# A hybrid decoder layer on one core: low halves of weights kept in DRAM for the second token half, gate operands made one step ahead, gather rates raised

## The chip, the cores and the metric

One core of a Trainium2 chip runs the whole layer. The metric is device time of one execution in microseconds, the median of three runs. Lower is better.

## What is computed

One decoder layer over 1024 tokens of width 1024, in float32:

- `x += concat(differential attention, mLSTM) @ w_out`, with four heads each; their inputs come from one projection `rms_norm(x) @ w_in` in 128-wide column blocks (29 of them with the gates' block).
- `x += PEER(rms_norm(x))`: per token and each of 8 retrieval heads, a query (`@ w_query`, 16 blocks) is matched with two sets of 128 keys; the best 16 of the 16 x 16 sums name 16 of 16384 experts. Each expert has a row of 1024 in `expert_u` and in `expert_v`: `y = sum_k g_k * gelu(x . u_k) * v_k`, so 128 experts per token.
- `x += sigmoid(rms_norm(x) @ w_ple_gate) * (p @ w_ple_proj)`, then a last RMSNorm.

## The kernel before

**Split numbers.** A float32 product is built of three matmuls. Each operand is split into a high half (ScalarE's copy to the rounded type `F32R`) and a low half (VectorE's subtraction of the high half). `mm3s` (line 140) issues hi x hi, hi x lo and lo x hi.

**Two token halves.** `front(0)` and `front(1)` (line 220) work on 512 tokens each: projection, attention, mLSTM, output projection, queries and top-k. Each of the two reads all 53 weight blocks of 512 KB (29 of `win`, 8 quarters of `wout`, 16 of `wq`) by `weight` (line 190), which loads the block on SP's queue, makes `whi` on ScalarE and `wlo` on VectorE. There are three buffers of `wraw` and two each of `whi` and `wlo`. In `project` and in the query stage all matmuls with the high half come ahead of those with the low half.

**The retrieval, done in two ways.** For 3 of the 8 token tiles the expert rows are gathered (`sparse`, line 831): 24 units of 16 steps; a step gathers one row per token of `expert_u` (`ru`, 512 KB) and of `expert_v` (`rv`) on GpSimd's queue and makes one pass over each on VectorE (lines 843 and 861), with the second table one unit behind the first: 400 steps. For the other 5 tiles it is dense: `dense_up` (line 944) multiplies with all of `expert_u` in 128 rows and applies Gelu into `ga_s` in DRAM; `gate_blocks` (line 891) builds the dense gate matrix `g_s` in DRAM; `dense_down` (line 1005) multiplies both and then with `expert_v`, four rows at a time in 32 groups. `tail` (line 1111) does the last part, a tile at a time in the order `TORD`; the last tile is tile 2, the last of the gathered ones, whose result it loads from `x3_s` (line 1124).

**Pacing.** The gathered part is a generator: 14 steps of top-k, then 400 steps. `pump(x)` (line 212) adds `x` to a debt and draws one step per whole number, at a lowered priority. It is called in the second token half only (`F_RATE`: per projection block, per query block but the last five, per output quarter), per row of the up stage (`UP_RATE`: the first value for 40 rows, then the second), per row of the down stage (`DOWN_RATE`), and in the tail until the generator is empty. `anchor` names an instruction, and `behind` orders the passes after it in the schedule without a semaphore. The rows gathered land in a ring of buffers, 3 deep in the front, 4 in the up stage, 6 in the down stage and 2 from row 108 of the down stage on (`FLUSH`).

**Gate products.** The last 42 of the top-k's steps take one row each of the up stage; from then on `gate_blocks` draws 80 steps, spread over the rows so that it ends near row 119. A block of 16 tokens is two steps: four VectorE operations make one-hot matrices (`o1`, `w0`, `o1` again, `o0`, lines 918 to 922, one buffer each), ScalarE reorders a half of them into `wc` (line 927, one buffer), TensorE makes 16 matmuls into `pg` (line 931), and ScalarE copies into `st` (line 934), which goes to DRAM when 32 tokens are full.

The order on each engine is made ahead of time by a scheduler that goes by priority (the order of the program, shifted by `high_priority`) and modelled times; on the chip each engine and queue then runs in that order.

## Time and profile before

| what | value |
|---|---|
| three runs | 3117.79, 3124.81, 3115.04 us; median 3117.79 |
| the profiled execution's own time | 3123.69 us |
| its span, first to last instruction | 3121.9 us |
| TensorE busy (matmul) | 2873.4 us, 92% |
| VectorE busy | 2557.4 us, 82% |
| ScalarE, GpSimd busy | 1317.8 us (42%), 1007.6 us (32%) |
| mean granted TensorE clock | 0.965 |
| moved by DMA | 829.01 MB, mean 266 GB/s |

Busy time is the time in which an engine executes instructions, whatever it waits for later; a matmul's end is modelled. The chain of waits goes back from the last instruction, at each step to what released it. The second token half runs from about 475 to 992 us of the span, the up stage to 1988, the down stage to about 2905, and the tail to the end.

### The profile page before, as it was taken

The page shows a single profiled execution, that of the slowest core. Times are in us where ns is not written, and L with a number is a line of the kernel's source. Part 1 is how long each engine was busy: PE and PEld are TensorE (multiplying, and loading weights), DVE is VectorE, ACT ScalarE, POOL GpSimd, SP SyncE. Part 2 cuts the span into 40 slices and gives each one's busy share as a digit, 9 for nine tenths or more (in the row PEclk, how much of TensorE's full clock was granted, in tenths as well). Part 3 has the DMA queues.
Part 4 walks back from the last instruction along what each step waited for, and adds up shares of the span by engine and source line. Part 5 has one row for each costly group of instructions (what it writes and reads, how often), then busy time and mean ns, then how long its engine had stood idle before and what let it go on. Part 6 is the DMA issues. An engine that isn't in the chain of part 4 may idle for free.

```text
span 3121.9 us, 44819 instructions
## 1 busy us (share of the span) xinstructions
PE 2873.4 (92%) x16367; PEld 2517.4 (81%) x16367; DVE 2557.4 (82%) x5349; ACT 1317.8 (42%) x2152; POOL 1007.6 (32%) x786
## 2 busy tenths in 40 slices
PE   7999989998697999999999999899989999998894
PEld 6887868776586999998889999778768888887773
DVE  5565889888799889799999797678778888888795
ACT  5664336655222222487776565212222222232241
POOL 0000000334414333444444555434333444414431
PEclk9999989999898999999999999899999999999997
DMA  5333433777846787899999989999989999988763
GB/s 168 100 111 127 150 126 93 233 229 244 303 133 233 264 276 244 306 345 340 343 340 346 370 328 367 372 348 340 313 291 330 339 333 329 338 295 276 259 222 124
DMA packets 316797, 829.01 MB, mean 266 GB/s; under 512 B 26144, under 2 KB 115104, under 8 KB 314016
## 3 DMA queue, kind: packets, MB, share of 16 engines
q0 software_dynamic: 112608, 410.04, 37.6%
q1 hardware_dynamic: 185536, 374.16, 34.9%
q10 hardware_dynamic: 18432, 41.95, 3.5%
q8 instruction: 128, 2.10, 0.3%
q14 instruction: 93, 0.76, 0.1%
HBM read 715.43 MB, written 102.24 MB: 262 GB/s over the span
## 4 chain that ended last, share of the span: by engine, by line
PE 55%; DVE 15%; DMA 12%; issue 12%; ACT 3%; POOL 2%; another core or an unknown queue 0%; SPq 0%; DVEq 0%; ACTq 0%; POOLq 0%
PE A L145 23%; PE mm L145 12%; PE keep L145 5%; DMA raw<-in_vr 4%; DMA rv<-in_ev,eidx 3%; DVE ya L861 3%; PE S L145 2%; DVE ru L843 2%; PE pg L931 2%; PE Y L136 2%; PE Y L137 2%; PE Y L138 2%; DVE tlo L881 1%; DMA ru<-in_eu,eidx 1%; POOL ru L827 1%
## 5 line engine op out<-in xcount | busy, mean ns | idle before, releaser
L827 POOL DMA_INDIRECT ru<-in_eu,eidx x384 | 508.4, 1324 | 1169.7 <-DVE ru L843 843.0
L827 POOL DMA_INDIRECT rv<-in_ev,eidx x384 | 491.2, 1279 | 443.5 <-DVE ya L861 286.8
L861 DVE SCALAR_TENSOR_TENSOR ya<-rv,cf,ya 128x1024 f32<-128x1024 f32 x384 | 492.3, 1282 | 46.5 <-DMA rv<-in_ev,eidx 29.3
L843 DVE SCALAR_TENSOR_TENSOR ru<-ru,sh 128x1024 f32<-128x1024 f32 x384 | 468.1, 1220 | 33.5 <-DMA ru<-in_eu,eidx 23.1
L881 DVE TENSOR_TENSOR tlo<-raw,thi 128x1024 fp32r<-128x1024 f32 x256 | 312.6, 1221 | 220.4 <-ACT thi L880 130.4
L880 ACT ACTIVATE thi<-raw 128x1024 fp32r<-128x1024 f32 x256 | 267.7, 1057 | 524.5 <-DMA raw<-in_vr 272.6
L145 PE MATMUL A<-ahi,thi 128*128 128x384 f32 x1024 | 348.7, 341 | 13.2 <-ACT thi L880 13.2
L145 PE MATMUL A<-alo,thi 128*128 128x384 f32 x1024 | 345.8, 338 | 0.0
L145 PE MATMUL mm<-ahi,whi 128*128 128x512 f32 (+1 forms) x752 | 301.4, 405 | 25.0 <-ACT ahi L236 13.1
L145 PE MATMUL mm<-alo,whi 128*128 128x512 f32 (+1 forms) x752 | 287.1, 394 | 7.1 <-DVE alo L237 7.1
L136 PE MATMUL Y<-thi,ph 128*128 128x512 f32 x640 | 250.2, 391 | 5.1 <-ACT thi L880 5.0
L145 PE MATMUL A<-xh,thi 128*128 128x256 f32 x1024 | 252.8, 284 | 0.7 <-ACT xh L971 0.7
L145 PE MATMUL A<-xl,thi 128*128 128x256 f32 x1024 | 252.7, 284 | 0.1
L137 PE MATMUL Y<-tlo,ph 128*128 128x512 f32 x640 | 250.0, 391 | 1.1 <-DVE tlo L881 1.0
L138 PE MATMUL Y<-thi,pl 128*128 128x512 f32 x640 | 249.4, 390 | 0.0
L1059 ACT ACTIVATE ph<-aq 128x640 fp32r<-128x640 f32 x128 | 87.3, 727 | 328.5 <-PE Y L137 309.4
L145 PEld LDWEIGHTS A<-ahi,thi 128*128 128x128 f32 x1024 | 193.6, 189 | 13.5 <-ACT thi L880 13.5
L145 PE MATMUL A<-ahi,tlo 128*128 128x384 f32 x1024 | 203.3, 337 | 0.0
L145 PE MATMUL keep<-tlo,ph 128*128 128x512 f32 x640 | 178.6, 403 | 22.7 <-DVE tlo L881 22.6
L145 PE MATMUL mm<-ahi,wlo 128*128 128x512 f32 (+1 forms) x752 | 193.9, 389 | 5.1 <-DVE wlo L196 5.0
L145 PEld LDWEIGHTS A<-xh,thi 128*128 128x128 f32 x1024 | 194.5, 190 | 1.0 <-ACT xh L971 0.9
L145 PEld LDWEIGHTS A<-xl,thi 128*128 128x128 f32 x1024 | 194.7, 190 | 0.3 <-DVE xl L972 0.3
(467 smaller groups left out, 6080.6 us busy)
## 6 DMA issues: line engine op xcount, KB each, us to landing
raw<-in_ut SPq DMA_DIRECT2D x128, 512.0 KB
raw<-in_vr SPq DMA_DIRECT2D x128, 512.0 KB
ga_s<-ga ACTq DMA_DIRECT2D x128, 320.0 KB
g_s<-st SPq DMA_DIRECT2D x20, 2048.0 KB
gq<-g_s SPq DMA_DIRECT2D x32, 1280.0 KB
aq<-ga_s SPq DMA_DIRECT2D x32, 1280.0 KB
wraw<-in_win SPq DMA_DIRECT2D x58, 512.0 KB
wraw<-in_wq SPq DMA_DIRECT2D x32, 512.0 KB
```

Of the source, the lines that this page charges most:

```text
L136: pe.matmul(o, lh, rh, start=start, stop=False)
L137: pe.matmul(o, lh, rl, start=False, stop=False)
L138: pe.matmul(o, ll, rh, start=False, stop=stop)
L145: pe.matmul(o, ll if p == "l" else lh, rl if p == "r" else rh, start=start and p == "h", stop=stop and n == last and p == names[-1])
L827: gp.indirect_dma_start(out=b, out_offset=None, in_=table, in_offset=bass.IndirectOffsetOnAxis(ap=eidx[part][:, i, k:k + 1], axis=0))
L843: behind(v.scalar_tensor_tensor(b, b, 1.0, st["h", tl], op0=OP.mult, op1=OP.mult, accum_out=st["d", n][:, j:j + 1]))
L861: op = v.scalar_tensor_tensor(ya, b, st["c", n][:, j:j + 1], ya, op0=OP.mult, op1=OP.add)
L880: sc.activation(hi, raw, AF.Copy)
L881: anchor(v.tensor_sub(lo, raw, hi.bitcast(F32)))
L931: pe.matmul(pg[:, b, :], o0[:, 4 * a + b, :], wc[:, c, a % 2, b, :], start=c == 0, stop=c == 1)
L1059: sc.activation(ph, av, AF.Copy)
```

## The change

Three things are changed.

1. In the first token half each low half is written to a DRAM tensor `lo_s` on GpSimd's queue. In the second half VectorE's subtraction is left out, and the low half is loaded from there on SP's queue, right behind the block's own load. There `wraw` has two buffers and `wlo` three. The anchor for the gathers' passes is then ScalarE's copy.
2. `gate_blocks` works on 8 tokens at a time, with two buffers of `o0` and `wc`; the products of a step are issued after the operands of the next have been made.
3. The rates: 1.8 to 1.9 per projection block, 0.9 to 1.2 per row in the first 40 rows of the up stage, 1.05 to 1.1 per row of the down stage.

```diff
@@ -68,10 +68,10 @@
 TORD = [4, 0, 5, 6, 7, 1, 3, 2]
 TAIL_RATE = 8.0
 TKEYS = [(0, q) for q in range(4)] + [(0, -1), (1, -1)] + [(1, q) for q in range(4)]
-F_RATE = (1.8, 1.3, 1.5)
-UP_RATE = (0.9, 1.45, 40)
+F_RATE = (1.9, 1.3, 1.5)
+UP_RATE = (1.2, 1.45, 40)
 QUIET = 5
-DOWN_RATE = 1.05
+DOWN_RATE = 1.1
 
 
 @with_exitstack
@@ -105,6 +105,7 @@
     x2_s = dram.tile([S // P, P, D], F32, name="x2_s")
     h2_s = dram.tile([S // P, P, D], F32, name="h2_s")
     x3_s = dram.tile([S // P, P, D], F32, name="x3_s")
+    lo_s = dram.tile([7 * H + 9 + 2 * PH, P, D], F32, name="lo_s")
     g_s = dram.tile([P // GB * NDT, P, P, GB], F32, name="g_s")
     ga_s = dram.tile([P, P, TD], F32, name="ga_s")
 
@@ -187,14 +188,19 @@
             v.scalar_tensor_tensor(fcs["nlam"], le[:, 1:2], -LAM0, le[:, 0:1], op0=OP.add,
                                    op1=OP.subtract)
 
-    def weight(wpool, src, shape):
-        raw = wpool.tile([P, 1024], F32, name="wraw", bufs=WR)
+    def weight(wpool, src, shape, part, n):
+        raw = wpool.tile([P, 1024], F32, name="wraw", bufs=WR - part)
         sy.dma_start(raw, src.rearrange("p a b -> p (a b)"))
         hi = wpool.tile([P] + shape, F32R, name="whi", bufs=2)
-        lo = wpool.tile([P] + shape, F32R, name="wlo", bufs=2)
-        sc.activation(hi.rearrange("p a b -> p (a b)"), raw, AF.Copy)
-        anchor(v.tensor_sub(lo.rearrange("p a b -> p (a b)"), raw,
-                            hi.rearrange("p a b -> p (a b)").bitcast(F32)))
+        lo = wpool.tile([P] + shape, F32R, name="wlo", bufs=2 + part)
+        hf, lf = (a.rearrange("p a b -> p (a b)") for a in (hi, lo))
+        if part:
+            sy.dma_start(lf.bitcast(F32), lo_s[n])
+            anchor(sc.activation(hf, raw, AF.Copy))
+        else:
+            sc.activation(hf, raw, AF.Copy)
+            v.tensor_sub(lf, raw, hf.bitcast(F32))
+            gp.dma_start(lo_s[n], lf.bitcast(F32))
         return hi, lo
 
     pumped = {"gen": None, "due": 0.0, "at": None}
@@ -227,7 +233,7 @@
             with pool(f"pa{part}", bufs=1) as pa:
                 hh = act.tile([P, DC, T], F32R, name="ahi")
                 hl = act.tile([P, DC, T], F32R, name="alo")
-                ready = {7 * H: weight(wp, win[7 * H], [DC, P])}
+                ready = {7 * H: weight(wp, win[7 * H], [DC, P], part, 7 * H)}
                 for dc in range(DC):
                     if dc % 2 == 0:
                         x2t = pa.tile([P, 2, T], F32, name="p", bufs=3)
@@ -236,7 +242,7 @@
                     sc.activation(hh[:, dc, :], xt, AF.Copy, scale=gcol[:, GMIX + dc:GMIX + dc + 1])
                     xlo = v.scalar_tensor_tensor(hl[:, dc, :], xt, gcol[:, GMIX + dc:GMIX + dc + 1],
                                                  hh[:, dc, :].bitcast(F32), op0=OP.mult, op1=OP.subtract)
-                ready[0] = weight(wp, win[0], [DC, P])
+                ready[0] = weight(wp, win[0], [DC, P], part, 0)
                 anchor(xlo)
                 if part == 0:
                     front_consts(fc)
@@ -289,7 +295,7 @@
 
                 def project(blk):
                     pump(F_RATE[0] * part)
-                    hi, lo = ready.pop(blk) if blk in ready else weight(wp, win[blk], [DC, P])
+                    hi, lo = ready.pop(blk) if blk in ready else weight(wp, win[blk], [DC, P], part, blk)
                     ps = mmp.tile([P, T], F32, name="mm")
                     mm3s([(ps, hi[:, dc, :], lo[:, dc, :], hh[:, dc, :], hl[:, dc, :], dc == 0, dc == DC - 1)
                           for dc in range(DC)], ("hr", "l"))
@@ -602,7 +608,7 @@
 
                 def out_quarter(blk, q, first, last):
                     pump(F_RATE[2] * part)
-                    hi, lo = weight(wp, wout[blk, q], [2, 512])
+                    hi, lo = weight(wp, wout[blk, q], [2, 512], part, 7 * H + 1 + 4 * blk + q)
                     mm3s(sum([out_terms(blocks[blk], hi, lo, q, i, first, last) for i in range(NT)], []),
                          ("hl", "r"))
 
@@ -647,7 +653,7 @@
                 out_quarter(1, 0, True, False)
                 out_quarter(1, 1, False, False)
                 pump(2 * F_RATE[2] * part)
-                lastq = [weight(wp, wout[1, q], [2, 512]) for q in (2, 3)]
+                lastq = [weight(wp, wout[1, q], [2, 512], part, 7 * H + 5 + q) for q in (2, 3)]
                 r2 = {}
                 for i in range(NT):
                     mm3s(sum([out_terms(blocks[1], *lastq[q - 2], q, i, False, q == 3) for q in (2, 3)], []),
@@ -692,7 +698,7 @@
                 pair = []
                 for hc in range(2):
                     pump(F_RATE[1] * part)
-                    pair.append((*weight(wp, wq[hc], [DC, P]), mmp.tile([P, T], F32, name="mm")))
+                    pair.append((*weight(wp, wq[hc], [DC, P], part, 7 * H + 9 + hc), mmp.tile([P, T], F32, name="mm")))
                 for cs in (slice(0, T // 2), slice(T // 2, T)):
                     for a in pair:
                         mm3s(query_terms(*a, cs), ("hl", "r"))
@@ -703,7 +709,7 @@
                         ps = pair[hc][2]
                     else:
                         pump(F_RATE[1] * part if hc < 2 * PH - QUIET else 0)
-                        hi, lo = weight(wp, wq[hc], [DC, P])
+                        hi, lo = weight(wp, wq[hc], [DC, P], part, 7 * H + 9 + hc)
                         ps = mmp.tile([P, T], F32, name="mm")
                         mm3s(query_terms(hi, lo, ps, slice(0, T)), ("hr", "l"))
                     qq = pb_.tile([P, T], F32, name="qq", bufs=2)
@@ -892,8 +898,25 @@
         ioe = gp_.tile([P, P, 4], F16, name="ioe")
         iof = load_const(iota_d[None, :].to_broadcast([P, P]), [P, P], "iof", gp_)
         v.tensor_copy(ioe, iof[:, :, None].to_broadcast([P, P, 4]))
-        sh = [P, 4, P, 4]
+        sh = [P, 2, P, 4]
         io = ioe[:, None].to_broadcast(sh)
+        prepared, held = [], {}
+
+        def gate_products(n, hb, sb, o0, wc):
+            if sb == 0:
+                held["st"] = gp_.tile([P, P, GB], F32, name="st", bufs=64 // GB)
+            st = held["st"]
+            for a in range(2):
+                pg = pG.tile([P, 4, P], F32, name="pg")
+                for b in range(4):
+                    for c in range(2):
+                        pe.matmul(pg[:, b, :], o0[:, 4 * a + b, :], wc[:, c, a, b, :], start=c == 0,
+                                  stop=c == 1)
+                t_ = sb * 8 + a * 4
+                sc.activation(st[:, :, t_:t_ + 4].rearrange("p j t -> p t j"), pg, AF.Copy, scale=1.0 / WSC)
+            if sb == GB // 8 - 1:
+                sy.dma_start(g_s[n * (P // GB) + hb], st)
+
         for n, tl in enumerate(DORD):
             part, i = divmod(tl, NT)
             fl = gp_.tile([P, 3, P], F32, name="fl", bufs=1)
@@ -907,35 +930,26 @@
             v.tensor_copy(it[:, 0:3], pt)
             v.tensor_tensor(it[:, 3], pt[:, 2], it[:, 2], op=OP.subtract)
             for hb in range(P // GB):
-                st = gp_.tile([P, P, GB], F32, name="st", bufs=64 // GB)
-                for sb in range(GB // 16):
-                    tb = slice(hb * GB + sb * 16, hb * GB + sb * 16 + 16)
+                for sb in range(GB // 8):
+                    tb = slice(hb * GB + sb * 8, hb * GB + sb * 8 + 8)
                     iv = [it[:, c, tb].rearrange("p (a b) -> p a b", b=4)[:, :, None, :].to_broadcast(sh)
-                          for c in range(4)]
-                    o0 = gp_.tile([P, 16, P], F16, name="o0", bufs=1)
+                          for c in range(1, 4)]
+                    o0 = gp_.tile([P, 8, P], F16, name="o0", bufs=2)
                     o1 = gp_.tile(sh, F16, name="o1", bufs=1)
                     w0 = gp_.tile(sh, F16, name="w0", bufs=1)
-                    v.tensor_tensor(o1, iv[1], io, op=OP.is_equal)
-                    v.tensor_tensor(w0, o1, iv[2], op=OP.mult)
-                    v.tensor_tensor(o1, o1, iv[3], op=OP.mult)
-                    v.tensor_tensor(o0, it[:, 0, tb][:, :, None].to_broadcast([P, 16, P]),
-                                    ioe[:, None, :, 0].to_broadcast([P, 16, P]), op=OP.is_equal)
-                    for a in range(4):
-                        if a % 2 == 0:
-                            wc = gp_.tile([P, 2, 2, 4, P], F16, name="wc", bufs=1)
-                            for c, w in enumerate((w0, o1)):
-                                sc.activation(wc[:, c], w[:, a:a + 2].rearrange("p a j b -> p a b j"), AF.Copy)
-                        pg = pG.tile([P, 4, P], F32, name="pg")
-                        for b in range(4):
-                            for c in range(2):
-                                pe.matmul(pg[:, b, :], o0[:, 4 * a + b, :], wc[:, c, a % 2, b, :], start=c == 0,
-                                          stop=c == 1)
-                        t_ = sb * 16 + a * 4
-                        sc.activation(st[:, :, t_:t_ + 4].rearrange("p j t -> p t j"), pg, AF.Copy,
-                                      scale=1.0 / WSC)
-                        if a % 2:
-                            yield True
-                sy.dma_start(g_s[n * (P // GB) + hb], st)
+                    wc = gp_.tile([P, 2, 2, 4, P], F16, name="wc", bufs=2)
+                    v.tensor_tensor(o1, iv[0], io, op=OP.is_equal)
+                    v.tensor_tensor(w0, o1, iv[1], op=OP.mult)
+                    v.tensor_tensor(o1, o1, iv[2], op=OP.mult)
+                    for c, w in enumerate((w0, o1)):
+                        sc.activation(wc[:, c], w.rearrange("p a j b -> p a b j"), AF.Copy)
+                    v.tensor_tensor(o0, it[:, 0, tb][:, :, None].to_broadcast([P, 8, P]),
+                                    ioe[:, None, :, 0].to_broadcast([P, 8, P]), op=OP.is_equal)
+                    if prepared:
+                        gate_products(*prepared.pop())
+                    prepared.append((n, hb, sb, o0, wc))
+                    yield True
+        gate_products(*prepared.pop())
 
     def chain(*gens):
         for g in gens:
```

## Rows read from the trace of the kernel before

**Rows 1.** Stages: start:end, length; busy PE, PEld, DVE, ACT, POOL; PEclk, DMA share, GB/s
```profile
0.00:475.00 475.00, 431.47 (x2234) 353.74 (x2234) 317.04 (x1241) 243.81 (x539) 5.68 (x14) 0.96 0.40 129
475.00:860.00 385.00, 332.44 (x1842) 275.95 (x1841) 330.37 (x746) 206.25 (x464) 116.81 (x98) 0.94 0.67 222
860.00:992.00 132.00, 109.45 (x535) 89.92 (x535) 131.28 (x689) 29.45 (x49) 30.57 (x22) 0.91 0.50 167
992.00:1292.00 300.00, 300.00 (x2055) 300.00 (x2055) 261.49 (x723) 88.51 (x142) 117.91 (x89) 1.00 0.80 275
1292.00:1646.00 354.00, 329.24 (x2658) 315.83 (x2657) 325.49 (x328) 275.20 (x322) 147.83 (x111) 1.00 0.90 330
1646.00:1988.00 342.00, 338.66 (x2580) 336.36 (x2579) 285.98 (x303) 197.62 (x255) 169.22 (x124) 1.00 0.95 358
1988.00:2345.00 357.00, 320.51 (x1379) 263.06 (x1378) 269.27 (x342) 77.15 (x97) 136.89 (x108) 0.94 0.95 329
2345.00:2776.00 431.00, 430.98 (x1898) 355.46 (x1897) 369.12 (x472) 107.05 (x132) 171.36 (x129) 1.00 0.96 332
...
2905.00:3060.00 155.00, 143.78 (x627) 115.22 (x625) 134.10 (x319) 52.06 (x97) 61.17 (x51) 0.96 0.71 234
```

**Rows 2.** Chain of waits, end of the span: start us, length us, what
```profile
3088.09 2.61 DMA x_s<-ya
...
3090.75 3.18 DMA x<-x_s
...
3093.98 1.97 PE tr L1139 x8
...
3110.24 0.70 ACT gt L1172
```

**Rows 3.** Waits from 2905 us on: total us, times, longest us
```profile
PE tr L1139 <- DMA x<-x_s: 34.0, 1, 34.0
```

**Rows 4.** VectorE groups from 2905 us on: busy us, mean ns | idle before
```profile
L861 DVE SCALAR_TENSOR_TENSOR ya<-rv,cf,ya 128x1024 f32<-128x1024 f32 x39 | 50.0, 1282 | 17.1 <-DMA rv<-in_ev,eidx 16.8
L843 DVE SCALAR_TENSOR_TENSOR ru<-ru,sh 128x1024 f32<-128x1024 f32 x22 | 26.8, 1218 | 7.1 <-DMA ru<-in_eu,eidx 7.1
```

**Rows 5.** VectorE groups, 475 to 860 us: the low halves
```profile
L196 DVE TENSOR_TENSOR wlo<-wraw,whi 128x1024 fp32r<-128x1024 f32 x35 | 42.6, 1217 | 7.0 <-ACT whi L195 3.1 <-issue 2.5 <-PE mm L145 0.6
```

**Rows 6.** VectorE groups, 860 to 992 us: the low halves
```profile
L196 DVE TENSOR_TENSOR wlo<-wraw,whi 128x1024 fp32r<-128x1024 f32 x13 | 15.8, 1212 | 0.0
```

**Rows 7.** Chain of waits, 475 to 860 us: shares by line; one piece
```profile
by line: PE mm L145 27.0%; PE S L145 10.6%; DMA dd<-qk 7.1%; issue 5.3%; PE S L413 5.2%; PE tr L441 4.7%; DVE ru L843 4.0%; DMA rv<-in_ev,eidx 3.4%; DMA ru<-in_eu,eidx 3.3%; PE tr L437 2.1%; DVE ya L861 1.9%; DVE wlo L196 1.6%; PE tr L540 1
...
775.16 13.11 DMA rv<-in_ev,eidx
```

**Rows 8.** Waits of TensorE, 475 to 860 us
```profile
PE tr L561 <- ACT t L366: 25.7, 2, 24.1
```

**Rows 9.** Chain of waits, whole span: transfers of 512 KB in loaded stretches
```profile
1412.92 8.58 DMA sh<-h_s
...
2306.36 13.32 DMA x_s<-ya
```

**Rows 10.** Chain of waits, 860 to 992 us: one weight block
```profile
883.18 5.51 PE mm L145 x24
```

**Rows 11.** GpSimd groups, 0 to 475 us
```profile
L234 POOL DMA_DIRECT2D p<-in_xT x4 | 2.1, 528 | 106.5 <-DVE alo L237 106.3 <-PE mm L145 0.2
```

**Rows 12.** TensorE groups, 1292 to 1646 us: the gate products
```profile
L931 PE MATMUL pg<-wc,o 128*128 128x128 f16 x816 | 62.5, 219 | 24.8 <-ACT wc L927 21.6 <-issue 2.4 <-DVE ya L861 0.4
```

**Rows 13.** Instructions of VectorE in order of time, from 1293.76 us
```profile
1293.76 1.22 DVE L918 TENSOR_TENSOR o<-it,ioe 128x2048 f16<-128x2048 f16 x1
1294.89 2.29 DVE L921 TENSOR_TENSOR o<-it,ioe 128x2048 f16<-128x2048 f16 x1
1297.09 1.22 DVE L919 TENSOR_TENSOR w<-o,it 128x2048 f16<-128x2048 f16 x1
```

**Rows 14.** VectorE groups, 992 to 1292 us
```profile
L792 DVE TENSOR_TENSOR i<-i,tmp 128x256 bf16<-128x256 bf16 x45 | 13.0, 288 | 0.8
```

## The prediction

> **What bounds the kernel now.** I read the busy time by stage first, then the chain of waits of each stage, then the groups of the engine that the chain names.
>
> The table by stage [rows 1] shows five regimes. In the first token half (0 to 475 us) TensorE is busy 431 of 475 us, GpSimd 6 us, and the DMA engines 0.40 of the time. In the second half (475 to 992 us) TensorE and VectorE share the bound: TensorE idles 52.6 us up to 860 and 22.6 us after it, and VectorE is busy 131.28 of the last 132 us. The up stage (992 to 1988 us) is TensorE's, without a gap up to 1292 us; from 1292 to 1646, where the gate products run, TensorE idles 24.8 us and VectorE is busy 325.49 of 354. The down stage begins with the DMA engines at 0.95 and TensorE short of work by 36.5 us, and then runs on TensorE alone (430.98 of 431) with the DMA engines at 0.96. The tail is TensorE's up to 3060 us.
>
> The end is something else. The chain's last pieces [rows 2] are the store of a tile's retrieval result, its load, and the transposes of that tile. TensorE waited 34.0 us for that load [rows 3], from 3060 to 3093.98 us; the gathers were not done. From 3093.98 to the end of the span are 27.9 us that the last tile needs in any case.
>
> **The count of gathered steps.** The generator has 14 steps of top-k and 400 of gathers, and a step is at most one row of each table (2 x 0.524 MB) and two VectorE passes, 1.22 and 1.28 us [rows 4], with 0.08 us for the accumulator 2.6 us together (an estimate). Before, the rates give 29 x 1.8 + 8 x 1.5 + 11 x 1.3 = 78.5 in the second half, 40 x 0.9 + 88 x 1.45 = 163.6 in the up stage, 128 x 1.05 = 134.4 in the down stage, and leave 37.5 for the tail. The trace agrees: from 2905 us on, 39 passes of the second table and 22 of the first are left [rows 4]. The change adds 2.9, 12 and 6.4: 21.3 steps move ahead of the tail and 16.2 stay.
>
> **Part by part.**
>
> The **tail**: 39 steps took from 2905 to about 3088 us, 4.7 us each. With 18 left they end near 2905 + 18 x 4.7 = 2989 us, and a store and a load of 2.61 and 3.18 us [rows 2] bring the tile by 2996, 64 us before TensorE asks for it. The wait goes whole: **-34 us**. What is late next is TensorE itself, busy 143.78 of 155 us there [rows 1]. The shorter queue behind VectorE may give back up to 8 of the 11 us that it idles; I take none.
>
> The **low halves, second token half**: 53 subtractions leave VectorE, 35 of them between 475 and 860 us (42.6 us, [rows 5]) and 13 after that (15.8 us, [rows 6]). In the stretch 860 to 992 VectorE is full, so up to 15.8 us could show; TensorE idles 22.6 us there, but part of that is the top-k behind the last query block, which stays. I take -10. From 475 to 860 the chain gives the subtraction itself 1.6% and the gathers' passes and transfers 12.6% [rows 7]; the largest hole of TensorE, 24.1 us [rows 8], stands behind a chain of tiny operations interleaved with gather passes, which wait for their rows (13.11 us in one, [rows 7]). Freeing 42.6 us of VectorE lets the passes run earlier, but doesn't shorten a gather. Bounds 0 and -40; I take -10, nearer to the chain's share. The 2.9 added steps put back 7.5 us of VectorE, inside the freed time. Together **-20**.
>
> The **loads** that replace them: 53 x 0.524 = 28 MB on SP's queue, behind each weight's own load, 54 GB/s over 517 us, which raises the 222 GB/s at a share of 0.67 [rows 1] to about 0.83. One load of 512 KB took 3.18 us in the quiet tail and 8.58 us in a stretch at 0.9; a store took 13.32 us [rows 2, 9]. Each weight comes every 385/35 = 11 us, and a third buffer lets the load start two weights ahead, 22 us; TensorE wants the low half only in the last third of a block of 24 matmuls (5.51 us, [rows 10]). So I cost it at 0, hidden by that lead; without it, see the first rival. The load also queues on SP ahead of the doubling transfers, 7.1% of the chain [rows 7], bound +0 to +10 us, taken within the 20.
>
> The **stores** in the first half: 53 issues on GpSimd's queue at 0.53 us [rows 11], 28 us on an engine busy 6 us [rows 1], 28 MB on DMA engines at 0.40. VectorE's next but one subtraction waits for the store; weights come every 475/58 = 8 us, so it has 16 us against 2.61 to 13.32. Cost 0, at most 53 x 0 to +5 us in all.
>
> The **gate operands**: TensorE idles 24.8 us before the gate products, 21.6 of it waiting for ScalarE's copies [rows 12]. One step ahead, the copies are made while the rows' own matmuls run. I take **-15** of the bounds 0 and -24.8. The split doubles VectorE's instructions, 4 more for each of 40 blocks of 16 tokens: 160. Their fixed cost: the 2048-wide pass takes 1.22 us, the 256-wide one of the same operation 0.288 [rows 13, 14], a line with 0.155 us at zero width; but successive starts stand 1.13 us apart for 1.22 and 2.20 for 2.29 [rows 13], so 0.09 is overlapped and 0.065 us is left. 160 x 0.065 = 10 us of VectorE, into some 28.5 us of its idle time from 1292 to 1646 us and 56 after it [rows 1].
>
> The Trainium skill, "VectorE: DVE Perf Modes", section "Side-by-side: where the cycles go for N=2048 bf16", gives each instruction some 150 cycles of start-up at 0.96 GHz and so 1224 ns for this width. The row's 1.22 us agrees; that all of it adds up does not, by the starts. By that rule, an estimate, the split would cost 25 us of VectorE in place of 10, and where VectorE decides the sum would be 3073 us.
>
> The **12 steps** added to the first 40 rows: 31 us of VectorE into the 38.5 us that it idles between 992 and 1292 us [rows 1]. TensorE has no gap there, so nothing can be gained, and whatever does not fit shows, 0 to +31. The gathers are placed last and can slide into the next rows; I take **+6**.
>
> The **down stage**: 6.4 steps, 6.7 MB, 20 us at 332 GB/s if the DMA engines were the bound; TensorE is full there, so **+3** (bounds 0 and +20). The pause at the change of rings stays as it is.
>
> Sum: -34 - 20 - 15 + 6 + 3 = **-60 us**. The profiled execution took 3123.69 us, 5.9 above the median of the runs; 3123.69 - 60 = 3063.7, on the median's scale 3117.8 - 60 = **3058 us**, own range 3030 to 3085.
>
> **The rivals.**
>
> First, **late low halves** (slower). SP works in order: if it stands in another wait while a low buffer comes free, the load starts late. Held until a block's start, it has only the first two passes of the block as cover, some 3.7 of its 5.51 us [rows 10], against 8.58 us: 4.9 us late. This decides once SP issues less than 5 us ahead. For a quarter of the 53 weights that is 64 us, and the front's 20 is gone: 3118 - 34 - 9 + 3 + 64 = 3142 us. For it: the 28 MB fall where the DMA engines are busiest in the front. Against: 11 us between weights. 0.10.
>
> Second, **only the tail gains**: the front is paced by gathers and doubling transfers [rows 7, 8], and the gate products by VectorE's throughput: 3118 - 34 + 3 = 3087 us. 0.22.
>
> Third, **VectorE becomes the bound of the up stage**: 31 us of steps and 10 of splitting find no room, since 261 and 325 us of work stand in 300 and 354: 3118 - 34 - 20 - 15 + 31 + 10 + 3 = 3093 us. For it: VectorE runs in order and stops at each late row. Against: 123 us of idle time in the whole stage. 0.15. By the page's rule above this rival would come to 3108.
>
> Fourth, **all of it shows**: front -40, gates -25, tail -34 and -8: 3118 - 107 = 3011 us. 0.13. The forecast keeps 0.40.
>
> **How the numbers follow.** A measurement here can tell 0.3%, 9.4 us: below 3108.4 is faster, above 3127.2 slower. Faster: 0.40 + 0.13 + 0.19 of the second + 0.10 of the third = 0.82. Same: 0.03 + 0.04 = 0.07. Slower: 0.10 + 0.01 = 0.11. The range 3015 to 3104 holds the forecast, the second, most of the third and half of the fourth.
>
> **What would show it.** Right: no wait of TensorE for the last tile's load, about 18 passes of the second table after the start of the tail, no subtraction of low halves after 475 us and a second half shorter by some 20 us, the gate products' idle time under 10 us, the first 40 rows of the up stage as long as before. Wrong: TensorE waiting for low halves that a DMA brings, SP's queue held by their buffers, low-half passes of the up stage late behind gathers, or a down stage whose full stretch slows from its 431 us.

## The result, and the profile after

The changed kernel takes 3096.29 us, the median of four runs (3093.41 to 3097.4); the ratio to the kernel before is 0.9922, with a 95% interval of 0.9907 to 0.9937. The kernel before took 3118.52 us in the same rounds. That is 22 us faster: inside the range, right in sign, but 38 us above the forecast of 3058. The profiled execution went from 3123.69 to 3095.2 us, so 28.5 us are there to be found in the trace against 60 forecast.

Three marks cut every run here into front, middle and tail: the first activation of tile ga (the up stage begins), the last add into aq (the last tile of the down stage leaves), and the end of the span. The tail wins what it should; front and middle win nothing.

| part | before, us | after, us | forecast | measured |
|---|---|---|---|---|
| front, 0 to first ga | 993.1 | 995.7 | -20 | +2.6 |
| middle, first ga to last aq | 1880.1 | 1885.8 | -6 | +5.7 |
| tail, last aq to the end | 248.7 | 211.9 | -34 | -36.8 |

The table by stage of the kernel after (stretch, length, then busy time with count of instructions for PE, PEld, DVE, ACT and POOL, then granted clock, DMA share and GB/s), to be held against [rows 1]:

```profile
475.00:860.00 385.00, 337.66 (x1748) 275.88 (x1748) 302.84 (x805) 205.32 (x464) 122.34 (x102) 0.92 0.80 277
860.00:994.00 134.00, 124.42 (x673) 105.68 (x672) 123.67 (x668) 36.72 (x59) 31.44 (x25) 0.97 0.70 243
994.00:1294.00 300.00, 300.00 (x2055) 300.00 (x2054) 287.05 (x777) 88.64 (x142) 145.82 (x112) 1.00 0.87 315
1294.00:1636.00 342.00, 327.53 (x2646) 315.21 (x2645) 325.14 (x422) 275.89 (x322) 142.14 (x108) 1.00 0.92 335
1636.00:1981.00 345.00, 344.75 (x2627) 343.43 (x2625) 298.25 (x371) 196.19 (x254) 181.59 (x133) 1.00 0.93 350
1981.00:2023.00 42.00, 7.72 (x64) 7.51 (x62) 12.07 (x15) 5.69 (x10) 15.14 (x15) 0.64 1.04 384
2023.00:2345.00 322.00, 303.44 (x1296) 248.67 (x1297) 260.07 (x331) 73.08 (x90) 123.08 (x93) 0.96 0.96 333
2345.00:2776.00 431.00, 425.23 (x1850) 345.35 (x1849) 369.61 (x472) 104.81 (x130) 179.18 (x136) 1.00 0.96 335
2914.00:3068.00 154.00, 140.99 (x621) 113.27 (x619) 103.50 (x268) 54.82 (x100) 18.96 (x17) 0.96 0.39 129
```

The reader sees the relief: VectorE has slack from 475 us on and a DMA share of 0.80 in place of 0.67; the 40 first rows of the up stage still last 300 us; the gate rows are 12 us shorter. And one new line: 42 us between the stages in which TensorE works 7.72 us.

**The tail** is as forecast. VectorE's groups from 2914 us on (lines of this kernel: L867 is the pass that was L861) show 18 passes of the second table where there were 39 [rows 4], and TensorE's longest wait in the same stretch is 4.9 us in place of 34.0 [rows 3]:

```profile
L867 DVE SCALAR_TENSOR_TENSOR ya<-rv,cf,ya 128x1024 f32<-128x1024 f32 x18 | 23.1, 1282 | 16.5 <-DMA rv<-in_ev,eidx 16.4
```

```profile
PE acc L146 <- DVE al L1156: 4.9, 1, 4.9
```

**The gate rows.** TensorE's group of gate products from 1294 to 1636 us idles less ([rows 12]: 24.8), though not under the 10 us that the prediction had asked for:

```profile
L913 PE MATMUL pg<-wc,o 128*128 128x128 f16 x807 | 61.6, 220 | 14.4 <-ACT wc L945 13.8
```

All rows of the up stage together take 992.5 us from the first to the last ga, against 1012.7 before. But the last prepared product is now issued behind the last row. The chain from 1970 to 2030 us (start, length, what) puts its store and then a load that stood ready before in the open, and TensorE's waits from 1975 to 2030 us give the sum (total, times, longest; in the second fence the first line is of the kernel after, the other two are of the kernel before in the same window):

```profile
1990.45 10.54 DMA g_s<-st
...
2001.48 18.02 DMA aq<-ga_s
```

```profile
PE keep L146 <- ACT thi L886: 34.3, 1, 34.3
PE keep L145 <- ACT ph L1059: 7.8, 1, 7.8
PE keep L145 <- ACT thi L880: 7.3, 1, 7.3
```

So TensorE waits 34.3 us at this place where it waited 15.1, 19.2 us more, and the 20.2 us that the rows won are gone.

**The front.** The hole of 24.1 us [rows 8] is gone; TensorE's largest waits from 475 to 996 us are

```profile
PE S L419 <- ACT kab L275: 8.2, 4, 4.1
PE tr L507 <- ACT jb L450: 6.7, 1, 6.7
```

and yet the up stage starts later, because the first half ends later. VectorE's waits from 330 to 440 us show a wait that was not there, a subtraction for the store of an earlier low half; the order of TensorE's instructions near 445 us (start, length, what, and in brackets the idle time before it) shows it arriving at a weight block; and the transposes of the query blocks of the first half, which ended with a start at 433.5 us before, end at 451.7 (first and last start; the kernel after, then the kernel before):

```profile
DVE wlo L202 <- DMA lo_s<-wlo: 15.6, 4, 4.1
```

```profile
445.56 3.78 PE L146 MATMUL mm<-ahi,wlo 128*128 128x512 f32 x8 [4.97 <-DVE wlo L202]
```

```profile
L719 PE MATMUL tr<-sk,qq x128: 272/275/580, 342.0 to 451.7; 128*128 128x128 f32 x128
L713 PE MATMUL tr<-sk,qq x128: 272/275/377, 339.2 to 433.5; 128*128 128x128 f32 x128
```

These query blocks take 109.7 us from the first to the last start, against 94.3: 15.4 us more, near the 15.6 us that VectorE waits for the stores.

### The profile page after: what moved, and what is told of

It reads as the page before. It is cut to its first block, busy times and chain, and to the rows that moved or that the text cites. A ratio compares the mean times of both kernels' runs of the same rounds, so it can differ in the third digit from the quotient of the medians.

```text
span 3093.4 us, 45112 instructions
## 1 busy us (share of the span) xinstructions
PE 2880.7 (93%) x16367; PEld 2518.4 (81%) x16367; DVE 2510.5 (81%) x5456; ACT 1318.7 (43%) x2152; POOL 1040.9 (34%) x839
## 4 chain that ended last, share of the span: by engine, by line
PE 56%; DVE 14%; DMA 13%; issue 10%; ACT 5%; POOL 1%; SPq 0%; ACTq 0%; DVEq 0%; POOLq 0%
PE A L146 25%; PE mm L146 9%; DMA raw<-in_vr 5%; PE keep L146 4%; DVE ya L867 3%; PE acc L146 2%; PE S L146 2%; PE pg L913 2%; DVE tlo L887 2%; DVE aq L1072 2%; PE Y L137 2%; DVE ru L849 2%; PE Y L138 2%; PE Y L139 1%; DMA rv<-in_ev,eidx 1%
## 5 line engine op out<-in xcount | busy, mean ns | idle before, releaser
L833 POOL DMA_INDIRECT ru<-in_eu,eidx x384 | 488.1, 1271 | 972.2 <-DVE ru L849 709.8
L833 POOL DMA_INDIRECT rv<-in_ev,eidx x384 | 516.4, 1345 | 523.7 <-DVE ya L867 344.3
L867 DVE SCALAR_TENSOR_TENSOR ya<-rv,cf,ya 128x1024 f32<-128x1024 f32 x384 | 490.8, 1278 | 40.4 <-DMA rv<-in_ev,eidx 23.7
L139 PE MATMUL Y<-thi,pl 128*128 128x512 f32 x640 | 249.4, 390 | 0.0
L146 PE MATMUL keep<-thi,ph 128*128 128x512 f32 x640 | 175.0, 396 | 36.7 <-ACT thi L886 34.3
L146 PEld LDWEIGHTS A<-alo,thi 128*128 128x128 f32 x1024 | 195.0, 190 | 0.0
## 6 DMA issues: line engine op xcount, KB each, us to landing
g_s<-st SPq DMA_DIRECT2D x20, 2048.0 KB, 10.3
```

The source lines that it names most:

```text
L139: pe.matmul(o, ll, rh, start=False, stop=stop)
L146: pe.matmul(o, ll if p == "l" else lh, rl if p == "r" else rh, start=start and p == "h", stop=stop and n == last and p == names[-1])
L833: gp.indirect_dma_start(out=b, out_offset=None, in_=table, in_offset=bass.IndirectOffsetOnAxis(ap=eidx[part][:, i, k:k + 1], axis=0))
L867: op = v.scalar_tensor_tensor(ya, b, st["c", n][:, j:j + 1], ya, op0=OP.mult, op1=OP.add)
```

## The experiments

All twelve were timed in rounds with the kernel before, and each ratio is to its time in the same rounds (medians 3123.2 to 3124.7 us; 3118.5 in the rounds of the kernel after). The spans cut by the same three marks, in us, each from one profiled execution, which can lie some 5 us off the median (e5). "Flush" stands for the last gate product drawn inside the rows' loop (e4 below; not the constant `FLUSH`), "raised rates" for those of the three that have their new value:

| run | low halves | gates | raised rates | front | middle | tail | span | median |
|---|---|---|---|---|---|---|---|---|
| before | old | old | none | 993.1 | 1880.1 | 248.7 | 3121.9 | |
| after | DRAM | ahead | F, UP, DOWN | 995.7 | 1885.8 | 211.9 | 3093.4 | 3096.3 |
| e1 | DRAM | old | none | 993.2 | 1874.9 | 247.8 | 3115.9 | 3117.4 |
| e2 | old | ahead | none | 991.6 | 1878.3 | 249.4 | 3119.3 | 3119.5 |
| e3 | old | old | F, UP, DOWN | 1001.2 | 1885.1 | 210.1 | 3096.4 | 3095.6 |
| e4 | DRAM | ahead, flush | F, UP, DOWN | 998.3 | 1878.1 | 210.3 | 3086.7 | 3086.7 |
| e5 | DRAM, x on SP | ahead, flush | F, UP, DOWN | 997.6 | 1877.2 | 211.5 | 3086.3 | 3093.5 |
| e6 | zero, no load | ahead, flush | F, UP, DOWN | 986.0 | 1876.0 | 211.4 | 3073.4 | 3074.6 |
| e7 | old | ahead, flush | F, UP, DOWN | 998.5 | 1879.8 | 209.3 | 3087.6 | 3090.2 |
| e8 | DRAM, x on SP | ahead, flush | UP | 987.8 | 1852.5 | 213.1 | 3053.4 | 3056.7 |
| e9 | as e8, 3 buffers | ahead, flush | UP | 978.2 | 1848.8 | 211.9 | 3038.9 | 3042.2 |
| e10 | old | ahead, flush | UP | 992.2 | 1849.6 | 214.8 | 3056.6 | 3059.2 |
| e11 | DRAM | ahead | UP | 992.4 | 1875.5 | 212.1 | 3080.0 | 3083.0 |
| e12 | old | old | UP | 993.1 | 1861.8 | 215.9 | 3070.8 | 3074.9 |

**Each part alone: e1, e2, e3.** e1 is the kernel after with the old gate_blocks and these rates, e2 the kernel before with the new gate_blocks, e3 the kernel before with the new rates.

```diff
-F_RATE = (1.9, 1.3, 1.5)
-UP_RATE = (1.2, 1.45, 40)
-DOWN_RATE = 1.1
+F_RATE = (1.8, 1.3, 1.5)
+UP_RATE = (0.9, 1.45, 40)
+DOWN_RATE = 1.05
```

> The kernel before with the low halves kept in DRAM, old rates and old gate operands. Theory A (the front gains nothing from the change because of the low halves' own transfers): the up stage starts within 10 us of before (985 to 1003 us, against 993), the last tile still waits for the gathers, and the time is 3110 to 3130 us. Rival B (the raised front rate, 2.9 more steps, ate the gain): without it the front is 15 to 25 us shorter, the up stage starts near 973 us and the time is 3095 to 3105 us.

Measured: ratio 0.9984 [0.9974, 0.9994]. The low halves alone leave the start of the up stage where it was (993.2 us) and the last tile still late. The two sides of this can be told apart at the last query transposes of the first half. The last of these starts at 455.3 us, 21.8 later than before, and from there to the up stage it is 537.9 us, against 559.6 before: 21.7 less, with the loads in it.

> The kernel before with the gate operands made one step ahead, old rates, no low halves in DRAM. Theory A (the last gate product, issued after the last row, opens the seam between the up and the down stage): the up stage's 128 rows take 15 to 25 us less than before (985 to 997 us from the first Gelu to the last, against 1012), TensorE stands some 30 us at the seam, and the time is 3120 to 3140 us. Rival B (the seam's hole comes from more gathers in the queues, that is from the raised rates): no hole over 15 us, time 3095 to 3108 us.

Measured: 0.9985 [0.9974, 0.9996]. The rows shrink from 1012.7 to 987.6 us (991.6 to 1979.2), the hole of TensorE between the stages is 33.7 us against 15.1, and the middle is 1878.3 us against 1880.1: next to nothing is left of the rows' gain.

> The kernel before with the three rates raised and nothing else. Theory A (the tail's gain is the rates' alone and VectorE has room for the 12 steps): no wait for the last tile's load, tail some 37 us shorter, up stage longer by at most 10 us, time 3078 to 3092 us. Rival B (the raised rates only pay with the VectorE time that the other parts free): up stage longer by 20 us or more, time 3100 to 3115 us.

Measured: 0.9909 [0.989, 0.9928]. The rates alone give the change's whole gain, though the time falls between the two theories. The tail's wait goes, but front (+8.1) and middle (+5.0) grow. In the front a new wait of TensorE from 717 to 1002 us stands behind passes of the gathers, which lie between the tiny operations that it waits for:

```profile
PE tr L671 <- DVE r_h L126: 13.1, 1, 13.1
```

**The hole between the stages: e4.** The last product is drawn inside the rows' loop.

```diff
-            nb, done = 16 * NDT, 0
+            nb, done = 16 * NDT + 1, 0
```

> The changed kernel, with the last gate product drawn inside the row loop, near row 118, instead of after the last row. Theory A (that product's store of 10.5 us and the loads behind it are the hole of 34 us at the seam): the hole shrinks to what before had, under 16 us, and the time falls by 18 to 34 us, to 3062 to 3078 us. Rival B (the hole is the DMA queues' filling at the change of stages): the hole stays over 25 us and the time within 8 us of 3096.

Measured: 0.987 [0.9846, 0.9894]. From 1975 to 2030 us TensorE now waits

```profile
PE keep L146 <- ACT thi L886: 18.3, 2, 9.8
```

So the hole shrinks from 34.3 us to 18.3, near the 15.1 of the kernel before, but the middle by 7.7 only, and the time stays above theory A's range. That the hole is the last product's is shown; why closing it pays half its length here is taken up below.

**Three tries on the front: e5, e6, e7.** e5 moves the x loads of the second half from GpSimd's queue, where 18 stores stand ahead of them, to SP's (of the two lines that are edited, one is shown); e6 replaces the loads of low halves by one constant tile (the lines that make it are left out); e7 is the kernel after, flush and all, with the old weight().

```diff
-                        (gp if part else sy).dma_start(x2t, xT[part, :, dc:dc + 2, :])
+                        sy.dma_start(x2t, xT[part, :, dc:dc + 2, :])
```

> The run with the last gate product drawn in the loop, and in it the second half's loads of x on SP's queue instead of GpSimd's. Theory A (GpSimd's queue holds those loads behind 18 stores of low halves that wait for VectorE): the loads go out some 100 us earlier, the last query blocks and the half change come 8 to 14 us earlier, the up stage starts at 984 to 991 us (998 there), and the time falls from 3087 to 3073 to 3080 us. Rival B (the late half change is made good later, since VectorE and the gathers set the front's end): the up stage starts within 4 us of 998 and the time is within 6 us of 3087.

Measured: 0.9904 [0.9879, 0.993]. The edit did not do what it was meant to: on SP's queue the x loads went out from 453.4 us on, against 448.8 in e4, so that my theory was not tested. The front is 997.6 against 998.3 us.

```diff
+        if part:
+            anchor(sc.activation(hi.rearrange("p a b -> p (a b)"), raw, AF.Copy))
+            return hi, fcs["zero"].rearrange("p (a b) -> p a b", b=shape[1])
```

> The run with the last gate product drawn in the loop, where the second token half takes a constant zero tile for every low half of the projection, output and query weights: neither subtraction nor load (that term of the product is left out of the result). The stores of the first half stay. Theory A (the 28 MB of loads on SP's queue slow the projections): the stretch from the last query block of the first half to the last projection (437 to 752 us there, 315 us; 291 before the change) takes 288 to 300 us, and the time is 3062 to 3078 us. Rival B (the projections are slowed by the late half change and by where the gathers then fall): that stretch stays at 308 to 320 us and the time within 6 us of 3087.

Measured: 0.9841 [0.9817, 0.9866]. Without the 53 loads the front is 12.3 us shorter (986.0 against e4's 998.3), and all of it comes behind the last query transposes of the first half: 530.6 us from there to the up stage against 544.2. The loads are not free.

> Raised rates, gate operands one step ahead and the last gate product drawn in the loop, with the low halves made by VectorE in both halves as before. Theory A (keeping the low halves in DRAM nets nothing: what VectorE gains at the end of the front is paid at the half change and in the projections): the time is 3078 to 3096 us, as with them (3087). Rival B (VectorE's 64 us are worth having once the rates are raised): 3100 to 3112 us.

Measured: 0.9888 [0.9864, 0.9912], 3090.2 us against e4's 3086.7. At the raised rates too the low halves in DRAM are worth next to nothing, front 998.3 against 998.5 us. Behind the last query transposes they win 22.1 us here (544.2 against 566.3), as in e1, and lose 21.9 ahead of them.

**The rates apart: e8, e10, e11, e12.** e8 is e5, e10 is e7 and e11 is the kernel after, each with F_RATE and DOWN_RATE back at 1.8 and 1.05; e12 is the kernel before with one number changed:

```diff
-UP_RATE = (0.9, 1.45, 40)
+UP_RATE = (1.2, 1.45, 40)
```

> As the run with x on SP's queue, with the front's and the down stage's rates back at 1.8 and 1.05 (only the first 40 rows of the up stage keep 1.2). Theory A (the gathers end some 75 us before they are needed, so 9 steps can be left to the tail, where nothing waits for them, and the full front and down stages get shorter): the last pass of the second table comes near 3030 us, ahead of the last tile's transposes, the down stage is 5 to 9 us shorter and the time is 3060 to 3074 us. Rival B (those steps cost nothing where they are): within 5 us of the run with x on SP's queue, or above it by a new wait for the last tile.

> Without the low halves in DRAM: gate operands one step ahead, last gate product in the loop, and of the raised rates only the 1.2 of the first 40 rows. Theory A (the low halves net nothing, and the overshoot of the other two rates costs some 30 us whatever the front does): 3052 to 3066 us. Rival B (the gain of the lower rates came from the low halves' freed VectorE): 3075 to 3092 us.

> The changed kernel with two of its three rates put back (1.8 in the front, 1.05 in the down stage). Theory A (those 9.3 steps cost more where they were put, some 3 us each, than they save in the tail, which waits for nothing either way): 3060 to 3074 us, no wait for the last tile's load, down stage 8 to 18 us shorter. Rival B (the last query-stage and seam effects hide it): 3085 to 3098 us.

> The kernel before with only the rate of the first 40 rows raised, 0.9 to 1.2. Theory A (12 steps in the stretch where VectorE has room remove the whole wait for the last tile): the up stage as long as before within 5 us, the down stage as before, the wait of 34 us gone or under 5, time 3072 to 3088 us. Rival B (12 steps don't suffice, the last tile still waits 10 us or more): 3090 to 3105 us.

Measured: e8 0.9784 [0.9761, 0.9807], e10 0.9799 [0.9781, 0.9817], e11 0.9871 [0.9853, 0.9888], e12 0.9845 [0.9824, 0.9867]. The 12 early steps alone (e12) take 51 us off the span, more than the whole change: 26 passes are left for the tail, and TensorE's longest wait there is 4.6 us. VectorE's group and TensorE's first wait from 2890 us on, of e12:

```profile
L861 DVE SCALAR_TENSOR_TENSOR ya<-rv,cf,ya 128x1024 f32<-128x1024 f32 x26 | 33.3, 1281 | 18.9 <-DMA rv<-in_ev,eidx 18.9
PE acc L145 <- DVE al L1142: 7.7, 3, 4.6
```

The rest of the change adds 23 us to that: e11, with the gates and the low halves, is 9.2 us longer than e12 (its 3083.0 us lie between its two theories), and the kernel after, with the two other raises, 13.4 longer than e11. By parts, from before over e12 and e11 to after: the middle goes -18.3, +13.7, +10.3, the front 0, -0.7, +3.3, the tail -32.8, -3.8, -0.2. In the front e8 is 4.6 us under e11, from which it differs there in the x loads alone; at the raised rates the same edit gave 0.7 (e5 against e4).

Why the middle behaves so is read from one window, from the end of the 40 first rows to the last aq add (columns as above). Before, e12, e3, the kernel after and e10, in this order:

```profile
1293.00:2873.00 1580.00, 1507.00 (x8869) 1341.92 (x8868) 1328.38 (x1544) 681.76 (x836) 654.37 (x494) 0.98 0.93 333
```

```profile
1293.00:2855.00 1562.00, 1504.06 (x8875) 1340.65 (x8874) 1328.85 (x1544) 683.00 (x836) 659.68 (x494) 0.98 0.94 337
```

```profile
1301.00:2886.00 1585.00, 1509.17 (x8886) 1337.37 (x8885) 1341.17 (x1562) 681.42 (x836) 686.00 (x506) 0.99 0.93 336
```

```profile
1296.00:2882.00 1586.00, 1506.62 (x8886) 1339.73 (x8885) 1352.60 (x1722) 682.18 (x836) 671.12 (x506) 0.98 0.94 336
```

```profile
1292.00:2842.00 1550.00, 1502.81 (x8884) 1340.58 (x8883) 1339.09 (x1704) 683.01 (x836) 660.35 (x494) 0.99 0.95 339
```

Length by GB/s gives the bytes: 526 MB before and in e12 and e10, 533 in e3 and after. In the first four TensorE's work is the same within 5 us; what differs is its idle time, 58 to 79 us, at a DMA share of 0.93 to 0.94. All fourteen kernels fall into these two classes: every one with DOWN_RATE 1.05 moves 525 to 527 MB here, every one with 1.1 moves 531 to 533. The 6.4 steps of the down stage are these 6.5 MB, 19 us at 336 GB/s, and e3 pays 23 us against e12. (F_RATE was lowered together with DOWN_RATE in these pairs, neither alone; F_RATE's steps fall ahead of this window.) The bytes are not all: at the same 526 MB the middle of e9 is 31 us shorter than that of before. ScalarE's waits for the down stage's weights (total, times, longest), of e3 from 2011 to 2884 us and of e12 from 2003 to 2852, show where:

```profile
ACT thi L880 <- DMA raw<-in_vr: 295.6, 59, 17.4
```

```profile
ACT thi L880 <- DMA raw<-in_vr: 249.0, 61, 13.7
```

The same pacing would explain e4 (argued from these rows): a hole that closes brings TensorE earlier to weights that the DMA engines have yet to bring. What speaks for it is that the flush is worth 7.7 us of the middle where the 6.5 MB are there (e4 against the kernel after) and 23.0 us where they are left away (e8 against e11, which differ in the x loads too). There gates with flush do pay: e10 against e12, which differ in nothing else, have a middle shorter by 12.2 us and a time of 3059.2 against 3074.9; and without the flush (e11, with low halves in DRAM) it is longer by 13.7 than e12's. So in e2, which has the old rates, it is mainly the hole that takes the rows' gain: behind the last row e2 takes 23.3 us more than before, 18.6 of them in the hole.

**A third low buffer in the first half: e9,** which is e8 and

```diff
-        lo = wpool.tile([P] + shape, F32R, name="wlo", bufs=2 + part)
+        lo = wpool.tile([P] + shape, F32R, name="wlo", bufs=3)
```

> The run with x on SP's queue and the front's and down stage's old rates, with a third buffer of the low halves in the first token half too. Theory A (there VectorE's subtraction waits for the store of the low half two weights before, about 4 us in every third query block, and makes the half change 10 to 13 us late): the waits of VectorE for the stores go, the last query block of the first half ends at 424 to 429 us (436 there), the up stage starts 5 to 13 us earlier than 988 and the time is 3042 to 3052 us. Rival B (the lateness is made good by the front's end): the first half ends earlier, but the up stage starts within 4 us of 988, and the time is within 5 us of 3057.

Measured: 3042.22 us, 0.9743 [0.9725, 0.9762], the best of all, 81 us under the kernel before in the same rounds. VectorE's waits from 330 to 440 us no longer hold the store; what is left at the top is

```profile
DVE wlo L202 <- ACT whi L201: 6.1, 1, 6.1
```

The transposes of the first half's queries end with a start at 439.8 us (451.7 in e8). From the first to the last start they take 95.0 us, where e8 takes 109.2 and before took 94.3, and the front is 9.6 us shorter than e8's:

```profile
L719 PE MATMUL tr<-sk,qq x128: 272/275/377, 344.8 to 439.8; 128*128 128x128 f32 x128
```

## Why the prediction was right or wrong

**Tail, -34: right,** -36.8. The count of steps (18 passes left) and the deadline at 3060 us held. But I took all 21 steps as needed: e12 shows that 12 suffice.

**Stores of low halves, "cost 0, at most 53 x 0 to +5 us in all": wrong.** I gave the store two weight periods, 16 us, by the mean of one weight per 8 us (475/58; the first half has 53 blocks, so 9.0 us). At the query blocks weights come in pairs: in the kernel after subtractions start at 400.65, 401.99 and 407.57 us, the last after a wait of 4.11 us for a store. Part 6 of the profile's page, DMA issues, after gives a median of 5.1 us from issue to landing, so the mean would have been no trouble. The stretch of the query transposes grows by 15.4 us, and the third buffer takes back 14.2 of them (e9 against e8). The last of them slip by 18.2 us; e9 takes back 11.9, and 5.6 of the rest stand already at the first of them (344.8 us against 339.2), which stays open.

**Loads, "cost it at 0, hidden by that lead": wrong** by 12 us (e6 against e4). Whether by the DMA engines' share of 0.80 or by their place in SP's queue was not told apart; the second half's third buffer of `wraw`, which the change takes away, was not tried either. From 440 us on one single wait of TensorE's matmuls names them, for 0.7 us, so the first rival, late low halves, did not come.

**Low halves of the second half, -20: right for the second half, lost at the end of the first.** The hole of [rows 8] vanishes, and e1 wins 21.7 us behind the last query transposes of the first half, with the loads paid; but its up stage starts at 993.2 us, since those transposes end 21.8 us later: their own stretch grows by 16.0, where the stores are waited for, and the first of them starts 5.8 later, which stays open. With the store's wait gone and F_RATE as before (e9, which has the x loads on SP's queue too) the front is 14.9 us shorter than before, near the 20.

**F_RATE's raise, "inside the freed time": wrong** by +8.1 and +6.3 us without the freed time (e3 against e12, e7 against e10), and with it by +3.3 (after against e11) and +9.8 (e5 against e8). Fronts with the same code and rates differ by up to 2.7 us (after and e4), so the sign is clear and the size is not.

**Gates, -15: near in its stage and missed in the sum.** The rows win 20.2 us, but not by the gates alone: these win 25.1 by themselves (e2), the early steps 10.3 by themselves (e12), and on top of the early steps the gates win 7.6 (e11) to 13.5 (e10). Then the hole between the stages costs 19.2. I moved the last product past the loop and did not count its store and the load behind it, two transfers of 10.54 and 18.02 us: a term put at nothing. The step was there to be seen: the generator's last line is drawn only when the rows are done.

**Splitting, 10 us of VectorE: right.** In VectorE's order of time after (start, length, what) a pass of half width takes 0.68 us and the next starts 0.60 us later:

```profile
1334.01 0.68 DVE L942 TENSOR_TENSOR w<-o,it 128x1024 f16<-128x1024 f16 x1
1334.61 1.22 DVE L946 TENSOR_TENSOR o<-it,ioe 128x1024 f16<-128x1024 f16 x1
1335.75 0.68 DVE L943 TENSOR_TENSOR o<-o,it 128x1024 f16<-128x1024 f16 x1
```

Two halves then take 1.20 us against 1.13 for the whole [rows 13], 0.07 us for each added instruction and 11 us for 160. The whole shows it too: e10's row above has 160 instructions of VectorE more than e12's and 10.2 us more busy time. The start-up of some 150 cycles in the Trainium skill, "VectorE: DVE Perf Modes", section "Side-by-side: where the cycles go for N=2048 bf16", fits the length of one pass but does not add up over passes in a row; by it, an estimate, the split would have cost 25 us.

**12 early steps, +6:** 0. VectorE takes them into its idle time (261 to 287 us busy of 300), TensorE has no gap. So the third rival, VectorE as the bound of the up stage, did not come. Beyond that e12's middle is 18 us shorter than before with the same bytes; why those flow at 337 in place of 333 GB/s was not settled.

**Down stage, +3, "TensorE is full there": wrong.** The upper bound, 20 us by bytes, was the value: the middle grows by 23.3 us without the gates (e3 against e12), by 30.2 and 24.7 with gates and flush (e7 against e10, e5 against e8), and by 10.3 in the kernel after (against e11). Behind the last row of the up stage alone it is 24.2, 20.8, 19.1 and 12.6. Why it is less in the kernel after, where both have the hole, was not settled. A full stretch of 431 us hid a start of the stage that is not full [rows 1].

By steps: front 22.6 us worse than forecast, middle 11.7 worse, tail 2.8 better, together the 31.5 us between -60 and -28.5. The number, 3096.3 us, is nearest to the third rival's 3093, and that by luck, since its mechanism did not come. The second rival's 3087 (only the tail gains) is near in the parts, but not by its reasons: front and gates did gain, and gave it back to a buffer, to the raise of F_RATE, to two transfers and to 6.5 MB. That the time fell inside the range is luck in the same way: four terms put at or near nothing (stores, loads, F_RATE, the down stage) and one left out (the hole) ate most of what the front and the rows won.

## What to carry to other kernels

A tile that is also stored lives until its store has landed: give it one more buffer before asking what the store itself costs, and check the shortest distance between uses, not the mean. Where a stage stands near 0.94 of the DMA engines, price what is added by bytes too, whatever a full stretch of TensorE says. In a software pipeline, place the last prepared piece inside the loop, and shift paced work only as far as the deadline needs.

## What the runs showed that was not expected

The traffic from the gate rows to the end of the down stage keeps within 333 to 340 GB/s in all fourteen kernels, a stretch of 2%; its bytes tell DOWN_RATE, its length only in part. One constant, UP_RATE, was worth 1.6% on its own (e12), twice the whole change.
